# Retention's input projections for all tokens at once by Strassen's scheme, through DRAM

## The chip, the cores and the metric

The kernel runs on one core of a Trainium2 chip. The core's engines work in parallel, each through its own queue in order: PE (TensorE, matmuls), DVE (VectorE), ACT (ScalarE), POOL (GpSimd) and SP (SyncE, which here issues the DMAs). The metric is the device time of one execution in microseconds; less is better. The median of three runs stands for the kernel before: 2782.24 us (2781.03 to 2786.2).

## The reference

A trunk of two layers over 1024 tokens of width 1024, in float32. Layer 0 mixes tokens by sparse attention, layer 1 by retention; behind each stands a gated feed-forward network with a convolution over three tokens. The change is in layer 1's mixer:

```python
proj = h @ w_in                       # h = rms_norm(x), 1024 x 1024; w_in 1024 x 6144
q = rotary(proj[..., :dq].reshape(bsz, seq, B_HEADS, B_DK))          # 4 heads of 256
k = rotary(proj[..., dq:2 * dq]...) * (B_DK ** -0.5)
v = proj[..., 2 * dq:2 * dq + dv].reshape(bsz, seq, B_HEADS, B_DV)   # 4 heads of 512
g = proj[..., 2 * dq + dv:]
...                                   # per head: (q k^T, decayed) v, plus q times a state
ret = rms_norm(ret, out_g)
y = ret * silu(g)
return y @ w_out
```

The rotary step turns the two halves of each q and k by the angle of their token: x1 cos - x2 sin and x1 sin + x2 cos.

## The kernel before

Every float32 product is made of three matmuls. Each operand is split into a rounded high part and the rest (hh and hl, whi and wlo): ACT copies, DVE subtracts; the product is high x high, low x high and high x low (mm3, L123 to L125). Layer 0's feed-forward network, and both layers' in part, already multiply by Strassen's scheme with seven block products for eight: the tokens are halved, the width and the weight's columns too. The first two products (first_products) go to DRAM (pd), the other five (second_products' loop, in ffn_first) add them up; prep_b makes the combined weights on DVE, product (L753) issues the matmuls.

Retention works on one half of 512 tokens after the other, and in a half on four heads. For a head, rotary() projects q and k with proj_T and turns them out of PSUM with cs, the table of cosines and sines; tok_proj() projects v and g, tokens on the partitions. In the core of a head, S = q k^T for four blocks of keys is scaled by the decay and split into sTh and sTl; the value products v,sT follow (in the second half also q times the state, sth and stl); ACT squares the result with a sum, and a chain of single columns through DVE and POOL gives the factor that normalises it (L678 to L683). Sixteen transposes (L710) turn it to y, which is split again and multiplied by wb_out into x. The first half leaves the state k^T v in DRAM for the second; for it k is kept in kf and transposed (L691). Weights come by SP into two raw slots (wraw), in the order of a list (plan_weights), two ahead of their use.

What sets the order is a scheduler that places each engine's instructions in a list; on the chip each engine then takes its list in order and waits on semaphores. In the kernel before, the projections of head n+1 stand in PE's list among the core's steps of head n. Between the two halves of retention stands the beginning of layer 1's feed-forward network on the first half (ffn_whole, a generator); the end of the second half hands over to the rest of it.

Of the kernel before, what the change touches and what calls it, by code (L numbers as in the profile page):

```python
# [5 lines left out]
F32 = mybir.dt.float32  # L6
# [45 lines left out]
class Prog:  # L52
# [4 lines left out]
    def plan_weights(self, phases):  # L57
        i = self.ins
        seq = []
        for ph, a in phases:  # L60
# [3 lines left out]
            elif ph == "outproj":  # L64
                seq += [(i["wa_out"][m], 1024, a == 0) for m in range(8)]
            elif ph == "up":
                seq += [(i["wf_up"][0, c], 1024, True) for c in range(*a)]
            elif ph == "ret":
                for n in range(4):
                    if n == 0:  # L70
                        seq += [(i["wb_qk"][n * 4 + c], 1024, False) for c in range(4)]
                        seq += [(i["wb_vg"][n, 0, kk], 1024, False) for kk in range(4)]
                    seq += [(i["wb_vg"][n, 1, kk], 1024, False) for kk in range(4)]
                    if n < 3:
                        seq += [(i["wb_qk"][(n + 1) * 4 + c], 1024, False) for c in range(4)]
                        seq += [(i["wb_vg"][n + 1, 0, kk], 1024, False) for kk in range(4)]
                    seq += [(i["wb_out"][n, mm], 1024, False) for mm in range(4)]
        self.wseq, self.wready, self.wpos = seq, [], 0

# [479 lines left out]
    def rotary(self, hh, hl, oh, ol, keep=None):  # L559
        nc = self.nc  # L560
        p0 = self.proj_T(hh, hl)
        p1 = self.proj_T(hh, hl)
        cos, sin = self.cs[:, 0], self.cs[:, 1]
        for d, (a, b, op) in enumerate(((p0, p1, ALU.subtract), (p1, p0, ALU.add))):
            u, v = keep[:, d] if keep is not None else self.tmp(), self.tmp()
            nc.vector.tensor_tensor(u, a, cos, ALU.mult)
            nc.vector.tensor_tensor(v, b, sin, ALU.mult)
            nc.vector.tensor_tensor(u, u, v, op)
            nc.scalar.activation(oh[:, d], u, AF.Copy)
            nc.vector.tensor_tensor(ol[:, d], u, oh[:, d].bitcast(F32), ALU.subtract)  # L570

    def tok_proj(self, hh, hl):

        ps = [self.bank() for _ in range(4)]
        for kk in range(4):
            wh, wl = self.weight()
            for j in range(4):
                for k2 in range(2):
                    k = kk * 2 + k2
                    w_h, w_l = wh[:, k2 * 512:(k2 + 1) * 512], wl[:, k2 * 512:(k2 + 1) * 512]  # L580
                    a, b = hh[:, k, j * 128:(j + 1) * 128], hl[:, k, j * 128:(j + 1) * 128]
                    self.mm3(ps[j], a, b, w_h, w_l, k == 0, k == 7)
        return ps

    def retention(self, half, x, h=None, then=None, also=lambda n: None):
        nc = self.nc
        hh, hl = h or self.all_chunks(x, C_GMIX + 8)
        kz = self.l1.tile([128, 4, 4], F32, tag="kz", name="kz")
        kn = self.l1.tile([128, 4, 4], F32, tag="kn", name="kn")
        ke = self.l1.tile([128, 4, 4], F32, tag="ke", name="ke")  # L590
        tok = lambda i: self.tok[half][i]

        def scales():

            r2 = self.small(4)
            nc.vector.tensor_tensor(r2, tok(1), tok(1), ALU.mult)
            for dst, c, w in ((kn, K_A, r2), (kz, K_Z, r2), (ke, K_EG, tok(0))):
                nc.vector.tensor_tensor(dst, self.kc(c, 16).rearrange("p (n j) -> p n j", j=4),
# [730 lines left out]
```

## Time and profile before

| | |
|---|---|
| median of three runs | 2782.24 us |
| profiled execution, its own time | 2783.58 us |
| its span, first to last instruction | 2781.7 us |
| mean granted TensorE clock | 0.976 |
| PE / DVE / ACT busy | 2655.4 / 1866.9 / 1096.2 us |
| DMA, mean over the span | 118 GB/s |

The span lies 1.9 us inside the profiled execution's time. Busy shares are means over stages of different kinds, so the stages are read one by one, by windows. Matmuls overlap: one of 512 columns lasts 0.39 us in the trace while the next starts earlier, so PE's pace is read from a stretch of them. "Idle before" counts the time an engine waited ahead of a group of instructions, and names what ended the wait.

### The profile page before, as it was taken

The page shows a single profiled execution, that of the slowest core. Times are in us where ns is not written, and L with a number is a line of the kernel's source. Part 1 is how long each engine was busy: PE and PEld are TensorE (multiplying, and loading weights), DVE is VectorE, ACT ScalarE, POOL GpSimd, SP SyncE. Part 2 cuts the span into 40 slices and gives each one's busy share as a digit, 9 for nine tenths or more (in the row PEclk, how much of TensorE's full clock was granted, in tenths as well). Part 3 has the DMA queues.
Part 4 walks back from the last instruction along what each step waited for, and adds up shares of the span by engine and source line. Part 5 has one row for each costly group of instructions (what it writes and reads, how often), then busy time and mean ns, then how long its engine had stood idle before and what let it go on. Part 6 is the DMA issues. An engine that isn't in the chain of part 4 may idle for free.

```text
span 2781.7 us, 31410 instructions
## 1 busy us (share of the span) xinstructions
PE 2655.4 (95%) x11888; PEld 2174.3 (78%) x11888; DVE 1866.9 (67%) x2828; ACT 1096.2 (39%) x1552; POOL 265.2 (10%) x193
## 2 busy tenths in 40 slices
PE   8977789998999999999999999999998999999999
PEld 6755567887788877888888888888886888888887
DVE  6889999765988878744544445445447977777632
ACT  6545424663433333323333343323334554454210
POOL 2543234321000000000000000000000000000000
PEclk9988789999999999999999999999999999999999
DMA  5221035204465575422222223223222433337712
GB/s 196 76 73 53 2 98 182 99 20 138 160 212 189 193 261 176 150 63 90 84 84 87 88 83 122 76 84 98 77 76 84 144 107 108 119 106 286 234 59 87
DMA packets 110343, 328.34 MB, mean 118 GB/s; under 512 B 12400, under 2 KB 13808, under 8 KB 110192
## 3 DMA queue, kind: packets, MB, share of 16 engines
q1 hardware_dynamic: 110192, 326.34, 35.6%
q8 instruction: 93, 1.52, 0.2%
q14 instruction: 58, 0.48, 0.1%
HBM read 250.27 MB, written 72.35 MB: 116 GB/s over the span
## 4 chain that ended last, share of the span: by engine, by line
PE 77%; DVE 15%; DMA 4%; issue 2%; ACT 2%; POOL 0%; SPq 0%; DVEq 0%; ACTq 0%; POOLq 0%
PE bank L753 25%; PE bank L123 17%; PE bank L125 17%; PE bank L124 17%; DVE junk L406 5%; DMA gin<-ud 2%; DVE tkb L416 1%; PE bank L534 1%; DVE sc L385 1%; DVE tkt L417 1%; DMA wraw<-in_wf_up 1%; DVE T L731 1%; DVE wlo L731 1%; DVE xo L764 0%; DVE lg L490 0%
## 5 line engine op out<-in xcount | busy, mean ns | idle before, releaser
L87 ACT ACTIVATE whi<-wraw 128x1024 fp32r<-128x1024 f32 (+1 forms) x194 | 205.3, 1058 | 507.7 <-PE bank L124 262.2
L753 PE MATMUL bank<-T,whi 128*128 128x512 f32 x1072 | 337.5, 396 | 21.6 <-ACT T L730 15.0
L753 PE MATMUL bank<-B,whi 128*128 128x512 f32 x1056 | 328.1, 393 | 11.1 <-ACT B L730 4.1
L89 DVE TENSOR_TENSOR wlo<-wraw,whi 128x1024 fp32r<-128x1024 f32 (+1 forms) x151 | 185.8, 1231 | 214.1 <-ACT whi L87 209.0
L124 PE MATMUL bank<-g,whi 128*128 128x512 f32 x704 | 274.1, 390 | 0.0
L123 PE MATMUL bank<-g,whi 128*128 128x512 f32 x704 | 266.5, 392 | 7.5 <-ACT g L730 5.6
L125 PE MATMUL bank<-g,wlo 128*128 128x512 f32 x704 | 272.5, 390 | 0.5 <-DVE wlo L731 0.5
L753 PEld LDWEIGHTS bank<-T,whi 128*128 128x128 f32 x1072 | 203.8, 190 | 71.0 <-ACT T L730 17.1
L730 ACT ACTIVATE whi<-wraw 128x1024 fp32r<-128x1024 f32 (+2 forms) x153 | 145.1, 949 | 267.0 <-PE bank L124 133.1
L753 PEld LDWEIGHTS bank<-B,whi 128*128 128x128 f32 x1056 | 199.9, 190 | 54.8 <-ACT B L730 4.4
L731 DVE TENSOR_TENSOR wlo<-wraw,whi 128x1024 fp32r<-128x1024 f32 (+2 forms) x153 | 165.7, 1083 | 76.5 <-ACT whi L730 76.3
L753 PE MATMUL bank<-T,wlo 128*128 128x512 f32 x536 | 210.3, 394 | 0.0
L753 PE MATMUL bank<-B,wlo 128*128 128x512 f32 x528 | 205.2, 392 | 0.0
L124 PE MATMUL bank<-wlo,hh 128*128 128x512 f32 x512 | 199.3, 389 | 0.0
L125 PE MATMUL bank<-whi,hl 128*128 128x512 f32 x512 | 199.3, 389 | 0.0
L123 PE MATMUL bank<-whi,hh 128*128 128x512 f32 x512 | 198.7, 390 | 0.0
L123 PE MATMUL bank<-hh,whi 128*128 128x512 f32 (+2 forms) x480 | 188.7, 393 | 10.3 <-ACT hh L134 8.3
L124 PE MATMUL bank<-hl,whi 128*128 128x512 f32 (+2 forms) x480 | 186.5, 389 | 0.1
L125 PE MATMUL bank<-hh,wlo 128*128 128x512 f32 (+2 forms) x480 | 186.4, 389 | 0.0
L406 DVE TENSOR_SCALAR_CACHE_REDUCE junk<-sc,tkt 128x640 f16<-128x640 f32 (+1 forms) x192 | 181.3, 944 | 4.4
L764 DVE TENSOR_TENSOR xo<-xo,bank 128x512 f32<-128x512 f32 x128 | 86.7, 685 | 126.8 <-PE bank L125 126.8
L123 PEld LDWEIGHTS bank<-g,whi 128*128 128x128 f32 x704 | 132.2, 188 | 37.6 <-ACT g L730 7.8
(244 smaller groups left out, 5305.6 us busy)
## 6 DMA issues: line engine op xcount, KB each, us to landing
wraw<-in_wf_up SPq DMA_DIRECT2D x113, 512.0 KB, 3.6
ud<-cu SPq DMA_DIRECT2D x88, 512.0 KB, 2.7
gin<-ud SPq DMA_DIRECT2D x88, 512.0 KB, 4.5
wraw<-in_wb_vg SPq DMA_DIRECT2D x64, 512.0 KB, 3.5
wraw<-in_wf_dn SPq DMA_DIRECT2D x48, 384.0 KB, 3.6
wraw<-in_wb_qk SPq DMA_DIRECT2D x32, 512.0 KB, 3.6
wraw<-in_wb_out SPq DMA_DIRECT2D x32, 512.0 KB, 3.5
wraw<-in_wa_in SPq DMA_DIRECT2D x26, 512.0 KB, 4.0
```

Of the source, the lines that this page charges most:

```text
L87: nc.scalar.activation(hi[:, :n], raw[:, :n], AF.Copy)
L89: eng.tensor_tensor(lo[:, :n], raw[:, :n], hi[:, :n].bitcast(F32), ALU.subtract)
L123: mm(ps, ah, bh, start=first, stop=False)
L124: mm(ps, ah, bl, start=False, stop=False)
L125: mm(ps, al, bh, start=False, stop=last)
L385: nc.vector.scalar_tensor_tensor(sc[:, o:o + n], rl[:, :n], w, sc[:, o:o + n], op0=ALU.mult, op1=ALU.add)
L406: V.tensor_scalar(junk[:, :Ls[b]], scs[b], of(b), None, op0=op, op1=ALU.add, accum_out=cnt[:, b:b + 1])
L416: V.tensor_scalar(bit, cnt, TOPK - 0.5, float(1 << k), op0=ALU.is_lt, op1=ALU.mult)
L730: return (self.nc.scalar.activation(hi, raw, AF.Copy), self.nc.vector.tensor_tensor(lo, raw, hi.bitcast(F32), ALU.subtract))
L731: self.nc.vector.tensor_tensor(lo, raw, hi.bitcast(F32), ALU.subtract))
L753: self.nc.tensor.matmul(ps, u, v, start=first and k + i == 0, stop=k == 3 and i == 2, skip_group_check=not (first and last))
L764: self.nc.vector.tensor_tensor(o, a, b, op)
```

## The change

A new function, ret_inputs, computes q, k, v and g for all 1024 tokens between layer 0's feed-forward network and the core. The columns of q, k and g are 16 pairs of 128 and go through first_products and second_products, which is now a function of its own; the values keep the tokens on the partitions, so val_product multiplies with the tokens as the stationary operand, in two pairs of heads (vp). Results stand in DRAM: q, k in gd[0], silu(g) in gd[1], v in vd, products that wait in rp and vp, x in xr. The tokens' norm is now applied to x before the projections. The matmuls of the projections go from 2304 to 2016.

In the core, a head's q, k and v come by DMA into the two raw slots, in turn with the weights; DVE turns q and k out of the raw tile and writes part of it in place, and splits them. The gate is loaded into sg; the normalised result goes to rt by ACT and is multiplied by the gate after the transposes (L806). cs, kh, kl, qh and the others of the pool l1 lie where T1, T2, T4, B22 and T3, the token operands of the scheme, lay before. In layer 0's down projection the last group of weights is run for the first token half and then, loaded again, for the second.

```diff
@@ -66,16 +66,17 @@ plan_weights
             elif ph == "ret":
-                for n in range(4):
...
+                seq += [(self.ret_src(c)[0], 1024, False) for c in range(16)]
+                seq += [(i["wb_vg"][n, 0, kk], 1024, False) for n in (0, 2) for kk in range(4)]
+            elif ph == "retout":
+                seq += [(i["wb_out"][n, mm], 1024, False) for n in range(4) for mm in range(4)]
@@ -556,87 +557,181 @@
-    def rotary(self, hh, hl, oh, ol, keep=None):
+    def ret_inputs(self, x, tt, s3, B):
...
+        for _ in self.first_products(range(16), B, self.rp):
+            next(rest, None)
...
+        for vp in range(2):
+            a = [self.bank() for _ in range(4)]
+            for half in range(2):
+                for q in range(2):
+                    hi, lo = self.weight()
+                    self.val_product(a, hi, lo, B[half], q, half == 0, half == 1)
+                for j in range(4):
+                    t = self.tmp()
+                    nc.scalar.activation(t, a[j], AF.Copy)
+                    nc.sync.dma_start(self.vp[vp][j] if half == 0 else self.vd[2 * vp][0][j], t)
+
+        def done(c, cc):
+            n, j = c // 4, c % 4
+            for i in range(2):
+                if j % 2:
+                    nc.scalar.activation(cc[i], cc[i], AF.Silu)
+                nc.sync.dma_start(self.gd[j % 2][n * 4 + j // 2 * 2 + i], cc[i])
...
+        self.second_products(16, self.ret_src, ops, nxt, s3, self.rp, done)
+
+        for vp in range(2):
+            vs = [self.hp.tile([128, 2, 2048], F32, tag="h", name="va") for _ in range(2)]
...
+            pq = self.xp.tile([128, 8, 512], F32, tag="x", name="vpq")
+            uq = self.xp.tile([128, 8, 512], F32, tag="x", name="vuq")
...
+            def s1(q):
+                add(sl(s3t, q), sl(a11, q), sl(a21, q), ALU.subtract)
+                add(sl(a21, q), sl(a21, q), sl(a22, q))
...
+            s3t = uq[:, 4:].rearrange("p k t -> p (k t)")
...
+            run(d, s1, T1, True, False, lambda j, ps: add(pq[:, 4 + j], ps, pq[:, j]))
+            a = [self.bank() for _ in range(4)]
+            run(a, s2, T2, True, False, lambda j, ps: add(uq[:, j], ps, pq[:, j]))
+            run(d, s4, B22, False, True, give(2 * vp, 1, uq))
+            run(a, lambda q: sl(s3t, q), T3, False, False, give(2 * vp + 1, 1, pq[:, 4:]))
+            run(a, lambda q: sl(a22, q), T4, False, True, give(2 * vp + 1, 0, pq))
...
+    def val_product(self, ps, hi, lo, t, q, first, last):
+        for j in range(4):
+            for k2 in range(2):
+                k = 2 * q + k2
+                w = [v[:, k2 * 512:(k2 + 1) * 512] for v in (hi, lo)]
+                b = [t[:, i, k, j * 128:(j + 1) * 128] for i in range(2)]
+                for i, (u, v) in enumerate(((b[0], w[0]), (b[0], w[1]), (b[1], w[0]))):
+                    self.nc.tensor.matmul(ps[j], u, v, start=first and k + i == 0, stop=k == 3 and i == 2,
+                                          skip_group_check=True)
+
+    def retention(self, half, x, then=None, also=lambda n: None):
...
+        def raw_pair(srcs):
+            raw = self.wp.tile([128, 1024], F32, tag="raw", bufs=2, name="wraw")
+            for t, src in zip(two(raw), srcs):
+                nc.sync.dma_start(t, src)
+            return raw
+
+        def rotary(j, n, oh, ol, keep):
+            add = self.add
+            a, b = two(raw_pair([self.gd[0][n * 4 + j * 2 + d][:, t0:t1] for d in range(2)]))
+            u, v = keep[:, 0] if keep is not None else self.tmp(), self.tmp()
+            add(u, a, cs[:, 0], ALU.mult)
+            add(v, b, cs[:, 1], ALU.mult)
+            add(u, u, v, ALU.subtract)
+            self.split(oh[:, 0], ol[:, 0], u)
+            add(b, b, cs[:, 0], ALU.mult)
+            add(a, a, cs[:, 1], ALU.mult)
+            w = keep[:, 1] if keep is not None else b
+            add(w, b, a)
+            self.split(oh[:, 1], ol[:, 1], w)
...
+            for j in (0, 2):
+                raw = raw_pair([self.vd[n][half][j + i] for i in range(2)])
+                self.split(self.two(v, 0, j), self.two(v, 1, j), raw)
...
-            for j, ps in enumerate(self.tok_proj(hh, hl)):
-                nc.scalar.activation(sg[:, j], ps, AF.Silu, scale=tok(1)[:, j:j + 1])
+            for c in range(4):
+                nc.sync.dma_start(sg[:, c], self.gd[1][n * 4 + c][:, t0:t1])
...
-                nc.vector.scalar_tensor_tensor(sg[:, j], ps, f, sg[:, j], op0=ALU.mult, op1=ALU.mult)
+                nc.scalar.activation(rt[:, j], ps, AF.Copy, scale=f)
@@ -995,13 +1114,16 @@ down
+        if l == 0:
+            todo[-8:] = [(g0, n, m, (h,)) for h in range(2) for g0, n, m, _ in todo[-8:]]
@@ -1204,37 +1348,32 @@ run
             with tt as tt, s3 as s3:
-                x, h = self.ffn_first(x, tt, s3)
+                x, B = self.ffn_first(x, tt, s3)
+                self.ret_inputs(x, tt, s3, B)
...
+                x = [self.xp.tile([128, 8, 512], F32, tag="x", name="x") for _ in range(2)]
+                for h in range(2):
+                    for m in range(8):
+                        nc.sync.dma_start(x[h][:, m], self.xr[h][m])
+                self.retention(0, x[0])
                 last = self.ffn_whole(1, x)
-                self.retention(1, x[1], None, last)
+                self.retention(1, x[1], last, lambda n: self.mean_square(0) if n == 0 else None)
```

Three places in the lists of instructions, row by row. The first is DVE's list where the first half of retention starts. Before, the projections of head 0's k and v (kf out of a bank, L132 v) are turned and split in between the splits of further weights:

```order
L568 TENSOR_TENSOR kf<-kf,t_9916 128x512
L89 TENSOR_TENSOR wlo<-wraw,whi 128x1024
L568 TENSOR_TENSOR kf<-kf,t_9922 128x512
L570 TENSOR_TENSOR kl_9852<-kf,kh_9851 128x512 x2
L89 TENSOR_TENSOR wlo<-wraw,whi 128x1024 x3
L132 TENSOR_TENSOR v<-bank,v 128x512 x4
L641 SCALAR_TENSOR_TENSOR t_10070<-bank,kn,kon 128x128
```

Now there are two stretches. At the end of the columns the results are added into cu, and then value pair 0 begins with vuq (vuq<-va is s3t, wlo<-va the first combined weight):

```order
L860 TENSOR_TENSOR cu<-bank,t_12362 128x512
L860 TENSOR_TENSOR cu<-bank,t_12346 128x512
L860 TENSOR_TENSOR vuq<-va 128x1024 x2
L860 TENSOR_TENSOR va<-va 128x1024 x3
L827 TENSOR_TENSOR wlo<-va,whi 128x1024
L860 TENSOR_TENSOR va<-va 128x1024
L827 TENSOR_TENSOR wlo<-va,whi 128x1024
L860 TENSOR_TENSOR va<-va 128x1024
L827 TENSOR_TENSOR wlo<-va,whi 128x1024
```

and behind the last results of value pair 1 (vpq) head 0's k and q are turned, out of wraw:

```order
L860 TENSOR_TENSOR t_13143<-bank,vpq 128x512
L860 TENSOR_TENSOR t_13146<-bank,vpq 128x512
L860 TENSOR_TENSOR kf<-wraw,cs 128x512
L860 TENSOR_TENSOR t_13183<-wraw,cs 128x512
L860 TENSOR_TENSOR t_13199<-wraw,cs 128x512
L860 TENSOR_TENSOR t_13200<-wraw,cs 128x512
L860 TENSOR_TENSOR wraw<-wraw,cs 128x512
L860 TENSOR_TENSOR kf<-kf,t_13183 128x512
L860 TENSOR_TENSOR wraw<-wraw,cs 128x512 x2
L860 TENSOR_TENSOR t_13199<-t_13199,t_13200 128x512
L860 TENSOR_TENSOR wraw<-wraw,cs 128x512
L860 TENSOR_TENSOR kf<-wraw 128x512
```

The splits of weights that stood among the turns are gone from there, and the turns stand behind the last value results.

The second place is PE's list in the second half, at the end of head 0's value products. Before, the projections of g and the next head's v (hh,whi) and, behind the transposes, its q (whi,hh) stand there:

```order
L123 MATMUL bank<-hh,whi 128x512
L124 MATMUL bank<-hl,whi 128x512
L125 MATMUL bank<-hh,wlo 128x512
L710 MATMUL bank<-kon,sg 128x128 x16
L123 MATMUL bank<-whi,hh 128x512
L124 MATMUL bank<-wlo,hh 128x512
L125 MATMUL bank<-whi,hl 128x512
L123 MATMUL bank<-whi,hh 128x512
```

Now the value products, the transposes and the output products follow each other:

```order
L124 MATMUL bank<-v,sTh_14899 128x512
L125 MATMUL bank<-v,sTh_14899 128x512
L126 MATMUL bank<-v,sTl_14900 128x512
L804 MATMUL bank<-kon,rt 128x128 x16
L124 MATMUL bank<-y,whi 128x512
L125 MATMUL bank<-y,whi 128x512
L124 MATMUL bank<-y,whi 128x512
L125 MATMUL bank<-y,whi 128x512
L126 MATMUL bank<-y,wlo 128x512
```

Nothing stands between the square of the result and its transposes on PE now, nor between those and y's products.

The third place is DVE's list in the second half's head 0. Before, the state's split (stl) is followed by splits of weights and the normalising chain (s, sg):

```order
L135 SCALAR_TENSOR_TENSOR sTl_13240<-bank,kn,sTh_13239 128x128
L644 TENSOR_TENSOR sTl_13255<-t_13256,sTh_13254 128x128
L656 TENSOR_TENSOR stl<-t_13262,sth 128x512
L656 TENSOR_TENSOR stl<-t_13266,sth 128x512
L89 TENSOR_TENSOR wlo<-wraw,whi 128x1024 x4
L680 SCALAR_TENSOR_TENSOR s_13412<-s_13410,ke 128x1
L683 SCALAR_TENSOR_TENSOR sg<-bank,s_13414,sg 128x512
L680 SCALAR_TENSOR_TENSOR s_13433<-s_13431,ke 128x1
```

Now v's last split and the next head's turns (out of wraw) stand around the state's split:

```order
L827 TENSOR_TENSOR v<-wraw,v 128x1024
L860 TENSOR_TENSOR t_15021<-wraw,cs 128x512
L827 TENSOR_TENSOR stl<-t_14907,sth 128x512
L827 TENSOR_TENSOR stl<-t_14911,sth 128x512
L860 TENSOR_TENSOR t_15022<-wraw,cs 128x512
L860 TENSOR_TENSOR wraw<-wraw,cs 128x512
L860 TENSOR_TENSOR t_15038<-wraw,cs 128x512
L860 TENSOR_TENSOR t_15021<-t_15021,t_15022 128x512
L860 TENSOR_TENSOR wraw<-wraw,cs 128x512
```

The turns, which stood in a stretch of their own behind the chain, come ahead of it.

## Rows read from the trace of the kernel before

**Rows 1.** Page: busy time of each engine, and the chain by engine.

```profile
PE 2655.4 (95%) x11888; PEld 2174.3 (78%) x11888; DVE 1866.9 (67%) x2828; ACT 1096.2 (39%) x1552; POOL 265.2 (10%) x193
...
PE 77%; DVE 15%; DMA 4%; issue 2%; ACT 2%; POOL 0%; SPq 0%; DVEq 0%; ACTq 0%; POOLq 0%
```

**Rows 2.** Windows: stretch, length, busy us (instructions) of engines, clock, DMA share, GB/s.

```profile
705.00:990.00 285.00, 285.00 (x1251) 235.75 (x1251) 241.22 (x303) 110.65 (x112) 0.00 (x0) 0.99 0.59 192
990.00:1020.00 30.00, 24.91 (x101) 19.50 (x100) 18.38 (x20) 8.88 (x9) 0.00 (x0) 0.94 0.98 353
1245.00:2092.00 847.00, 844.68 (x3866) 702.74 (x3865) 405.82 (x599) 284.44 (x437) 22.17 (x35) 1.00 0.27 87
2130.00:2160.00 30.00, 24.24 (x90) 17.40 (x91) 28.02 (x34) 17.30 (x22) 0.00 (x0) 0.85 0.11 36
```

**Rows 3.** Groups by line, DVE, 705 to 990: count, busy us, mean ns, idle.

```profile
L859 DVE SCALAR_TENSOR_TENSOR cu<-cu,cols 128x1022 f32<-128x1022 f32 x25 | 32.0, 1280 | 0.0
```

**Rows 4.** Groups by line, PE in 1245 to 2092.

```profile
L123 PE MATMUL bank<-whi,hh 128*128 128x512 f32 x512 | 198.7, 390 | 0.0
L123 PE MATMUL bank<-hh,whi 128*128 128x512 f32 x256 | 99.8, 390 | 0.0
```

**Rows 5.** Timeline at the end of a head's value products: start, length, engine, operation.

```profile
1865.28 0.40 PE L125 MATMUL bank<-v,sTl 128*128 128x512 f32 x1
1865.52 0.39 PE L123 MATMUL bank<-hh,whi 128*128 128x512 f32 x1
...
1865.78 0.60 ACT L678 ACTIVATE t<-bank 128x512 f32<-128x512 f32 x1 [3.46 <-PE bank L125]
...
1866.27 0.19 ACT L678 ACTIVATION_READ_ACCUMULATOR t<-bank 128x1 f32 x1
...
1866.50 0.16 DVE L680 SCALAR_TENSOR_TENSOR s<-s,ke 128x1 f32<-128x1 f32 x1 [1.34 <-ACT t L678]
...
1866.80 0.54 POOL L139 TENSOR_TENSOR s<-s,nh 128x1 f32<-128x1 f32 x1 [2.44 <-DVE s L680]
...
1867.38 0.75 DVE L683 SCALAR_TENSOR_TENSOR sg<-bank,s,sg 128x512 f32<-128x512 f32 x1 [0.72 <-POOL s L139]
```

**Rows 6.** Timeline of DVE on a rotary.

```profile
1887.49 0.69 DVE L567 TENSOR_TENSOR t<-bank,cs 128x512 f32<-128x512 f32 x1 [3.30 <-PE bank L125]
1888.10 0.68 DVE L566 TENSOR_TENSOR t<-bank,cs 128x512 f32<-128x512 f32 x1
```

**Rows 7.** Groups by line and shape in 1245 to 2092: the split of a weight.

```profile
L89 DVE TENSOR_TENSOR wlo<-wraw,whi 128x1024 fp32r<-128x1024 f32 x126 | 154.3, 1225 | 194.2 <-ACT whi L87 192.9
L87 ACT ACTIVATE whi<-wraw 128x1024 fp32r<-128x1024 f32 x125 | 132.9, 1063 | 376.9 <-PE bank L124 203.0 <-PE bank L125 167.5 <-issue 4.5
```

**Rows 8.** DMA issues by kind: count, KB each, median us to landing.

```profile
ud<-cu SPq DMA_DIRECT2D x88, 512.0 KB, 2.7
...
wraw<-in_wb_out SPq DMA_DIRECT2D x32, 512.0 KB, 3.5
...
cs<-in_cossin SPq DMA_DIRECT2D x2, 512.0 KB, 4.1
```

**Rows 9.** DMA issues of the stretch 2510 to 2570.

```profile
gin<-ud SPq DMA_DIRECT2D x18, 512.0 KB, 6.4
...
ud<-cu SPq DMA_DIRECT2D x4, 512.0 KB, 8.0
```

**Rows 10.** Timeline of PE: a head's transposes.

```profile
1887.29 1.91 PE L710 MATMUL bank<-kon,sg 128*128 128x128 f32 x16
```

**Rows 11.** Timeline of PE after a wait.

```profile
1015.68 2.44 PE L123 MATMUL bank<-g,whi 128*128 128x512 f32 x6 [1.92 <-ACT g L730]
1017.92 0.63 PE L124 MATMUL bank<-g,whi 128*128 128x512 f32 x1
1018.35 0.63 PE L125 MATMUL bank<-g,wlo 128*128 128x512 f32 x1
...
1019.89 0.39 PE L125 MATMUL bank<-g,wlo 128*128 128x512 f32 x1
```

More of the change, by code (lines that the diff above doesn't have):

```diff
@@ L572, in tok_proj @@
[L572 to L583, printed above, removed]
@@ new lines, in val_weight @@
+    def val_weight(self, raw):
+        hi = self.wp.tile([128, 1024], F32R, tag="whi", bufs=3, name="whi")
+        lo = self.wp.tile([128, 1024], F32R, tag="wlo", bufs=3, name="wlo")
+        self.split(hi, lo, raw)
+        return hi, lo
+    def val_product(self, ps, hi, lo, t, q, first, last):
+        for j in range(4):
+            for k2 in range(2):
[5 more added lines that the diff above has]
+                                          skip_group_check=True)
@@ new lines, in retention, with qk, values @@
+    def retention(self, half, x, then=None, also=lambda n: None):
+        nc = self.nc
+        self.plan_weights([("retout", 0)])
+        cs = self.l1.tile([128, 2, 512], F32, tag="cs", name="cs")
+        nc.sync.dma_start(cs, self.ins["cossin"][half])
+        t0, t1 = half * H, half * H + H
+        two = lambda t: [t[:, i * 512:(i + 1) * 512] for i in range(2)]
+        def raw_pair(srcs):
[16 more added lines that the diff above has]
+            self.split(oh[:, 1], ol[:, 1], w)
+        def qk(n):
+            kf = self.hp.tile([128, 2, 512], F32, tag="h", name="kf") if half == 0 else None
+            r = []
+            for j in (1, 0):
+                oh = self.l1.tile([128, 2, 512], F32R, tag=("qh", "kh")[j], name=("qh1", "kh1")[j])
+                ol = self.l1.tile([128, 2, 512], F32R, tag=("ql", "kl")[j], name=("ql1", "kl1")[j])
+                rotary(j, n, oh, ol, (None, kf)[j])
+                r = [oh, ol] + r
+            return r + [kf]
+        def values(n):
@@ L886, in finish, with second_products @@
                 nc.sync.dma_start(self.ud[0][1][c], ub)
-        for c in range(NFF):
+        self.second_products(NFF, src, ops[0], nxt[0], s3, self.pd, done)
+        return self.down(0, tt, late)
+    def second_products(self, n, src, ops, nxt, s3, pd, done):
+        nc, add = self.nc, self.add
+        T1, T2, T4, B22, T3 = ops
+        cu = [self.xp.tile([128, 4, 1024], F32, tag="x", name="cu") for _ in range(2)]
+        held = None
+        def finish(p):
+            c, a, a22, p1, cc = p
+            self.product(a, a22, T4, False, True)
+            add(cc[1][:, :512], a, p1)
+            done(c, cc)
+        for c in range(n):
             s1, s2, s3_, s4, a22 = nxt
@@ L1051, in down, with inputs @@
                 nc.sync.dma_start(y[h][:, m], self.xd[l][h][m])
-        hs = None
+        B, more = None, iter(())
         ahead = []
-        for i, (g0, n, m) in enumerate(todo):
+        def inputs():
+            nonlocal B
+            self.mean_square(0)
+            yield
+            chunk = self.normaliser(y[0], C_GMIX + 8, 0)
+            for k in range(4):
+                chunk(k)
+            yield
+            B, ch = self.first_inputs(y[0])
+            next(ch)
+            yield
+            for k in range(4, 8):
+                chunk(k)
+            yield
+            yield from ch
+        for i, (g0, n, m, hs) in enumerate(todo):
             final = g0 + n == NFF
-            lag = l == 0 and final and m > 0
-            if i + 2 < len(todo) and not lag:
+            if i + 2 < len(todo):
                 dn(i + 2)
@@ L1206, in run @@
                     pass
-                for _ in self.first_products(range(NFF - PRE[0]), B):
+                for _ in self.first_products(range(NFF - PRE[0]), B, self.pd):
                     steps(3)
```

250 lines of the change are left out of this document (127 added, 123 removed).

## The prediction

> **What bounds the kernel now.** I read the page's busy shares and chain first [rows 1]: TensorE (PE) is busy for 2655.4 of 2781.7 us and carries 77% of the chain that ended last. The windows say whether that holds in the stages that the change touches [rows 2]. In 705 to 990 us, the old Strassen stage (layer 0's second products), PE is busy for all 285.00 us with 1251 matmuls: 285.00/1251 = 0.228 us from one 512-column matmul to the next. In 1245 to 2092, inside retention, it is busy for 844.68 of 847.00, so 2.3 us are idle, while VectorE (DVE) needs 405.82 and DMA 27%. The groups of that window [rows 4] hold 512 matmuls of the form whi,hh and 256 of hh,whi; each stands there on three lines, 768 x 3 = 2304: all the projections of q, k, v and g. So PE is the bound, the projections cost what their count costs, and they have a second office. The timeline at the end of a head's value products [rows 5] shows it: after the last v,sTl at 1865.28 the chain ACT square, ACT accumulator, DVE, POOL, DVE runs on until 1868.13, and PE spends that time on hh,whi, projection matmuls that need nothing of it.
>
> **What is removed.** 2304 matmuls become 384 + 192 (first products) and 960 + 480 (second products), 2016; 288 fewer x 0.228 = **65.7 us**. New first and second products have the shape of the stage at 705 to 990, where the same additions, splits and stores left PE no idle time, so I cost that arithmetic at nothing; the cover is PE's 60 matmuls (13.7 us) a column, and by DVE's 241.22 busy of 285 there is 15% left. Layer 0's conv, in which a line like that of [rows 3] stands for 32.0 us of that DVE time, is not in the new columns. If the cover fails, a column costs what DVE exceeds 13.7 us. The 2.3 us idle in the window go as well: **68.0 us** in all.
>
> **What is added: waits on PE.** Prices: 512-wide DVE operations in a row start 0.60 us apart (1887.49, 1888.10; the first lasts 0.69) [rows 6]; a 1024-wide one lasts 1.22, and in a row I take 1.14 (0.08 less, as at 512; an estimate); an ACT copy of 1024 lasts 1.06 [rows 7]. A store of 512 KB lands after 2.7 us, a 512 KB weight after 3.5, cs after 4.1 [rows 8]; in the burst of 2510 to 2570 loads of 512 KB take 6.4 and stores 8.0 [rows 9].
>
> (1) Columns to value pair 0. The last column's accumulation ends at E. The first DVE operation of the pair writes vuq, which has the slot of cu; it waits until the last gate's store has left it. Add (0.95 with its lag), two SiLUs of 1024 (2.1, by ACT's copy), then the store, with 2 MB of va loads ahead of it in SP's queue: 3.0 + 8.0 = E+11 by the burst, E+5.7 by the quiet row; I take E+8.5, between them, since half of those loads are released a column earlier. Then five adds before the first wlo, which is what the second matmul of each pair reads: 5 x 1.14 + 1.22 = 6.9, so E+15.4; matmuls that read only whi cover 1.8. **13** (10 to 16).
>
> (2) Pair 0 to pair 1: vuq again, now behind the last add: 0.95 + 6.9 - 1.8 = **6** (5 to 8).
>
> (3) Pair 1 to the core. cs takes the place of T4, which the last value product reads, so its load starts at E2 and lands at E2+4. Sixteen DVE operations of 0.60 follow for head 0's k and q (9.6), with two ACT copies between them: S's products, 3.8 us of PE work, end at E2+16, 12 lost. v's splits hold the value products 2 more. The weights of wb_out come last of all: two raw slots, in order, so they queue behind head 1's k, q and v. From the last ksl split on, DVE needs 7.5 us to free k's slot, 12.1 to q's last split, 13.3 to v's first; the load then freed lands 3.5 later and is split 1.06 later, at 18. PE has 2 us left there (8 matmuls): 16 lost. 12 + 2 + 16 = **30** (26 to 36). No row of before shows a core head without projections, so this is built, not seen.
>
> (4) Heads 1 to 3 of the first half: the state products stand beside the y chain; PE has 150 matmuls of 512 columns (30 value, 24 state, 96 output: 34.2), S 3.8 and 24 transposes at 0.12 (2.9) [rows 10], 40.9 us a head; DVE's operations of a head come to about 34 (rotary 9.6, sT 4.4, v and wlo 6 x 1.2, x 8 x 0.60, y with the gate 8 x 0.65, ksl 2). 2 each, **6** (0 to 12).
>
> (5) Second half, head 0: DVE's rotary stands behind the last x addition, and stl behind the rotary: q,k ends 12.5 after the last matmul and sth's products 21; less what PE does meanwhile, 16.5. The first wb_out weight again comes after v, 10.5 more. **27** (16 to 30).
>
> (6) Second half, heads 1 to 3. The y chain is uncovered: [rows 5] give 0.60 + 0.19 + 0.16 + 0.54 with gaps, 1.6 from the square's start at 1865.78 to the last step's at 1867.38, 0.3 ahead of it, and ACT's copy 0.6 behind it: 2.5; then the sixteen transposes, 1.91 [rows 10], are PE's own work; then DVE's gain, ACT's copy and DVE's rest of y, 1.7 to the first y matmul: 4.2 idle a head. stl now stands behind the rotary, 5.5 a head, in one head also behind eight normaliser operations. 3 x 4.2 + 5.5 + 10.5 = **29** (14 to 38).
>
> (7) Clock. Behind an idle 1.92 us matmuls of 0.63 stood 0.43 apart, and only 4 us later, from 1019.89, did they take 0.39 again [rows 11]; the granted clock of the stretch 990 to 1020 is 0.94, and of 2130 to 2160 0.85 [rows 2], between the levels 1.2 and 2.4 GHz as a mean. I add 1.5 for each of (1), (3) and (5), and 0.5 for the rest: **8** (2 to 14).
>
> Waits: 13 + 6 + 30 + 6 + 27 + 29 + 8 = **119 us** (73 to 154 if all ends come together).
>
> The Trainium skill, "TensorE: Matmul & The Clock Gate", section "HAM oscillation — how this bites in real kernels", says that a kernel whose matmul groups alternate with waits can start every group cold, paying the half clock again each time. The slow matmuls behind the 1.92 us of idle time agree. Without the rule term (7) would be some 3, the three long waits at 1 us each, and the time 2828; with it paid at every wait inside a head, the contention rival below.
>
> Other moves: the last group of layer 0's down projection runs all units of the first token half, then those of the second, with eight more weight loads (as those of 3.5 in [rows 8]) and x0's normalisation beside it. DVE has about 29 us of work there (8 units of 0.9 + 0.6 + 0.6, 8 gains of 0.6, 4 splits and 2 early weights of 1.2) for 33 of PE (144 matmuls): 0, at most 3. The new loads and stores of rp and gd run beside the columns, as pd and ud did at 705 to 990, with DMA at 59% and 192 GB/s there against 353 at 990 to 1020 [rows 2]: 0.
>
> Net: 119 - 68 = +51. Against the profiled execution's own 2783.58: 2834.6; the median of the runs, 2782.24, lies 1.3 under it, so **2833**.
>
> **Rivals.**
> - *Handovers only* (faster). DVE and ACT run ahead inside the core, as the scheduler's order lets them, so (4), (6) and the weights of (3) and (5) cost nothing: 13 + 6 + 14 + 16.5 + 4 = 54 against 68: -14, 2768. For it: DVE is busy for less than half of the retention window [rows 2]. Against it: the y chain is a chain of latencies, whoever has time. It decides if y's weights are split before the transposes end.
> - *All hidden* (faster): 2783.6 - 68 = 2715 or so, if PE finds other work at each place. After the change the order puts the products of the value step, the transposes and the y products next to each other, with nothing between: 1 in 30.
> - *Even*: waits of 63 to 74 us, within 0.2% (5.6 us, what a measurement of this kernel can tell from no change).
> - *Contention and clock* (worse): the 2 MB of x loads, vd, gd and weights at the handovers land at 8 us as in [rows 9], and the core's matmuls run at a mean clock of 0.85 as in 2130 to 2160: 323 x 0.15/0.85 = 57, less the 8 already in: 2833 + 49 = 2882. For it: clock follows waits in [rows 2]. Against: gaps of 2 to 5 us between groups of 20 us.
>
> **How the numbers follow.** Slower as worked out 0.72 (2800 to 2865 alone); contention 0.08; even 0.05; handovers only 0.12; all hidden 0.03. Faster 0.15, same 0.05, slower 0.80. The range takes in the ends of the seven terms and the handover rival: 2766 to 2870.
>
> **What would show it.** In the profile after: a PE busy time lower by 60 to 66 us; PE idle gaps of 10 us or more at three places (before the first value product, before the first S product of each half), each ended by DVE; cs landing after the last value product; PE's L804 waiting for ACT in heads 1 to 3 of the second half; PEclk under 0.9 in slices of the core. Wrong would be: the core's 323 us of matmuls (4 x 40.9 and 4 x 39.9) in less than 345 (then handovers only), or idle gaps within the columns (DVE's cover gone, slower than I say).

## The result, and the profile after

The change makes the kernel slower: median 2872.82 us (2868.34 to 2873.74, 4 runs) against 2783.44, a ratio of 1.0318 (95%: 1.03 to 1.0335). The forecast was 2833 with a range of 2766 to 2870: right in sign, 40 us short, and 2.8 us outside the range. The profiled execution takes 2871.95 us, its span is 2870.2.

The page after, in its busy shares and its granted clock, stands against [rows 1]:

```profile
PE 2631.9 (92%) x11616; PEld 2144.4 (75%) x11616; DVE 2011.2 (70%) x3036; ACT 1134.0 (40%) x1606; POOL 265.0 (9%) x193
...
PEclk9987889999999999999999897998899999999999
```

PE runs 272 matmuls fewer and yet is busy only 23.5 us less, and four slices of the clock row behind the middle stand at 7 or 8. Both runs agree within 0.5 us up to 1076 us and behind the end of retention. The windows of that stage answer to [rows 2] (columns as there), first of the kernel before:

```profile
1076.00:2123.90 1047.90, 1045.04 (x4755) 868.27 (x4753) 540.42 (x757) 350.27 (x514) 23.18 (x36) 1.00 0.30 94
```

Then of the kernel after, the whole stage and its parts (columns by Strassen's scheme; value pairs; first half's core; second half's core):

```profile
1076.00:2212.90 1136.90, 1020.10 (x4482) 836.24 (x4480) 683.24 (x963) 389.77 (x568) 22.86 (x36) 0.94 0.45 149
1240.00:1590.00 350.00, 350.00 (x1553) 289.74 (x1551) 199.38 (x255) 121.76 (x151) 1.01 (x1) 1.00 0.59 194
1590.00:1740.00 150.00, 124.76 (x523) 100.63 (x521) 71.26 (x80) 23.32 (x22) 0.00 (x0) 0.92 0.39 138
1740.00:1965.00 225.00, 179.11 (x792) 146.04 (x792) 136.43 (x236) 89.78 (x164) 9.44 (x16) 0.88 0.39 129
1965.00:2205.00 240.00, 194.86 (x850) 158.24 (x851) 148.85 (x247) 92.50 (x160) 11.41 (x18) 0.90 0.33 107
```

The stage grew by 1136.90 - 1047.90 = 89.0 us, the whole difference. Three sums make it up. **Work**: 1045.04/4755 = 0.2198 us a matmul before, a mean over wide and narrow ones; 4755 - 4482 = 273 fewer give -60.0. **Idle**: 1136.90 - 1020.10 = 116.8 after, 2.9 before: +113.9. **Clock**: 4482 x 0.2198 = 985.0, but PE was busy 1020.10: +35.1, which agrees with the records of the granted clock, half in 14 spells between 1606 and 2125 us that cost 33.6 us of busy time (half of what PE was busy in them; 1.5 to 3.5 each). The records show no such spell in this stretch of the kernel before. 113.9 + 35.1 - 60.0 = 89.0. In the columns PE has no idle time and the full clock: all the loss lies behind 1590.

PE's waits there (us in all, times, longest):

```profile
PE bank L124 <- ACT whi L88: 36.9, 4, 19.8
PE bank L668 <- ACT whi L826: 21.5, 4, 15.5
PE bank L124 <- ACT qh L826: 18.8, 2, 11.3
PE bank L125 <- DVE stl L827: 11.1, 3, 7.5
PE bank L124 <- ACT sth L826: 8.3, 4, 4.0
PE bank L125 <- DVE y L827: 8.3, 6, 3.3
PE bank L124 <- ACT y L826: 6.4, 6, 1.4
PE bank L804 <- ACT rt L777: 3.2, 5, 1.1
```

The releaser that the profile names is often the last link of a chain. The first long wait, in the timeline of all engines (start, length, engine, operation, in brackets the idle time before it and what ended it):

```profile
1600.83 2.23 SPq L609 DMA_DIRECT2D va<-in_wb_vg  x4
...
1603.18 0.35 SPq L599 DMA_DIRECT2D gd<-cu  x1
...
1611.70 2.36 DVE L860 TENSOR_TENSOR vuq<-va 128x1024 f32<-128x1024 f32 x2 [10.17 <-DMA gd<-cu]
...
1616.34 2.07 PE L668 MATMUL bank<-whi,T 128*128 128x512 f32 x4 [15.54 <-ACT whi L826]
```

The last gate's store stands behind four va loads of 512 KB in SP's queue and only when it has left its slot, 8.5 us after its issue began (1611.70 less 1603.18), may DVE write vuq, which lies there. The longest wait, 19.81 us ahead of head 0's output products, and what follows it:

```profile
1785.78 1.23 DVE L827 TENSOR_TENSOR v<-wraw,v 128x1024 fp32r<-128x1024 f32 x1 [2.81 <-ACT v L826]
1786.34 1.06 ACT L826 ACTIVATE v<-wraw 128x1024 fp32r<-128x1024 f32 x1 [0.59 <-DMA wraw<-vd]
1787.03 8.91 SPq L87 DMA_DIRECT2D wraw<-in_wb_out  x4
1790.64 1.06 ACT L88 ACTIVATE whi<-wraw 128x1024 fp32r<-128x1024 f32 x1 [3.25 <-DMA wraw<-in_wb_out]
1791.75 0.80 PE L124 MATMUL bank<-y,whi 128*128 128x512 f32 x1 [19.81 <-ACT whi L88]
...
1792.77 0.63 PE L124 MATMUL bank<-y,whi 128*128 128x512 f32 x1
...
1797.76 0.39 PE L124 MATMUL bank<-y,whi 128*128 128x512 f32 x1
```

The output weight's load is issued at 1787.03, when the first split of head 1's v (DVE, to 1787.01) gives a raw slot back. Behind the wait a matmul lasts 0.63 us until 1797, then 0.39. The windows on both sides show the two levels, 1.2 and 2.4 GHz:

```profile
1791.70:1797.00 5.30, 5.25 (x12) 4.13 (x13) 2.45 (x2) 1.42 (x2) 0.00 (x0) 0.50 0.47 134
1797.00:1805.00 8.00, 8.00 (x36) 6.59 (x35) 4.42 (x5) 1.75 (x2) 0.00 (x0) 1.00 0.56 186
```

### The profile page after: what moved, and what is told of

Its sections match the earlier page's. It is cut to its first block, busy times and chain, and to the rows that moved or that the text cites. A ratio compares the mean times of both kernels' runs of the same rounds, so it can differ in the third digit from the quotient of the medians.

```text
span 2870.2 us, 31665 instructions
## 1 busy us (share of the span) xinstructions
PE 2631.9 (92%) x11616; PEld 2144.4 (75%) x11616; DVE 2011.2 (70%) x3036; ACT 1134.0 (40%) x1606; POOL 265.0 (9%) x193
## 4 chain that ended last, share of the span: by engine, by line
PE 74%; DVE 17%; DMA 4%; issue 2%; ACT 2%; SPq 0%; POOL 0%; DVEq 0%; ACTq 0%; POOLq 0%
PE bank L849 35%; PE bank L125 11%; PE bank L126 10%; PE bank L124 10%; DVE junk L407 5%; PE bank L668 5%; DMA gin<-ud 1%; DVE tkb L417 1%; DVE t L860 1%; PE bank L535 1%; DVE tkt L418 1%; DMA wraw<-vd 1%; DVE x L835 1%; DVE sc L386 1%; DMA wraw<-in_wf_up 1%
## 5 line engine op out<-in xcount | busy, mean ns | idle before, releaser
L849 PE MATMUL bank<-B,whi 128*128 128x512 f32 x1440 | 445.4, 392 | 11.1 <-ACT B L826 4.1
L849 PE MATMUL bank<-T,whi 128*128 128x512 f32 x1344 | 419.5, 394 | 23.9 <-ACT T L826 16.0
L88 ACT ACTIVATE whi<-wraw 128x1024 fp32r<-128x1024 f32 (+1 forms) x122 | 128.5, 1053 | 260.0 <-PE bank L125 90.4
L849 PE MATMUL bank<-T,wb 128*128 128x512 f32 x864 | 213.9, 391 | 0.8 <-DVE cu L860 0.8
L860 DVE TENSOR_TENSOR cu<-bank,t 128x512 f32<-128x512 f32 x198 | 133.9, 686 | 112.4 <-PE bank L849 107.3
L849 PEld LDWEIGHTS bank<-T,wb 128*128 128x128 f32 x864 | 163.1, 189 | 35.3 <-DVE cu L860 1.2
L90 DVE TENSOR_TENSOR wlo<-wraw,whi 128x1024 fp32r<-128x1024 f32 (+1 forms) x79 | 97.6, 1238 | 115.6 <-ACT whi L88 112.0
L124 PEld LDWEIGHTS bank<-g,whi 128*128 128x128 f32 x704 | 132.1, 188 | 35.6 <-ACT g L826 6.5
L849 PEld LDWEIGHTS bank<-B,wlo 128*128 128x128 f32 x720 | 135.9, 189 | 28.3
L126 PEld LDWEIGHTS bank<-g,wlo 128*128 128x128 f32 x704 | 132.1, 188 | 28.6 <-DVE wlo L827 1.0
L125 PEld LDWEIGHTS bank<-g,whi 128*128 128x128 f32 x704 | 132.1, 188 | 27.5
```

The lines of the kernel that those rows point to most:

```text
L88: nc.scalar.activation(hi[:, :n], raw[:, :n], AF.Copy)
L90: eng.tensor_tensor(lo[:, :n], raw[:, :n], hi[:, :n].bitcast(F32), ALU.subtract)
L124: mm(ps, ah, bh, start=first, stop=False)
L125: mm(ps, ah, bl, start=False, stop=False)
L126: mm(ps, al, bh, start=False, stop=last)
L849: self.nc.tensor.matmul(ps, u, v, start=first and k + i == 0, stop=k == 3 and i == 2, skip_group_check=not (first and last))
```

## The experiments

Two theories stood against each other. *Waits*: each wait has its own cause in the order of a queue or in the reuse of a piece of memory, goes when that is undone, and the half clock is a second price of the same waits. *DVE and ACT as the bound*: behind 1590 DVE and ACT are the limit, and a wait taken away comes back at the next place. Ratios are to the kernel before, with 95% intervals; gains are to the changed kernel's 2872.8.

**One wait at a time.** a_s3late: S3 is made late and in place, so that the first DVE operation of a value pair no longer writes vuq.

```diff
-                add(sl(s3t, q), sl(a11, q), sl(a21, q), ALU.subtract)
...
+            def s3(q):
+                add(sl(a11, q), sl(a22, q), sl(a11, q), ALU.subtract)
+                return sl(a11, q)
```

> Value pairs only: S3 is no longer written first into the slot of cu (vuq) but made later, as a22 - S2 in place; nothing is left out. Theory W (the loss is PE's named waits, each with a spell of half clock behind it): the 15.5 us wait ahead of value pair 0 falls under 4 and its spell (3.2 us of PE time) goes with it, the 5.5 us wait ahead of pair 1 changes by less than 3; 2857 us (2850 to 2862). Rival (the burst of weight loads behind the columns is what is late, whatever DVE writes first): the wait stays at 10 or more, 2866 or above.

2848.36 us (2846.25 to 2850.76), 1.0229 [1.0212, 1.0246]: -24.5, more than expected, since the wait of 5.5 us ahead of pair 1 went too. The waits of L668 (21.5) are gone from the list whole; only 2.9 us came back, in two small waits (for cu and for sTh), and the half clock costs 4.8 us less (28.9). The window of the value pairs, 1590 to 1740, to set beside that of after:

```profile
1590.00:1740.00 150.00, 134.40 (x584) 110.28 (x583) 89.31 (x117) 33.79 (x46) 1.48 (x2) 0.94 0.50 175
```

b_wfirst: two output weights are loaded ahead of the next head's q and k, and v behind the second.

```diff
+            self.prefetch(self.wpos + 2)
             if n < 3:
...
-            if n < 3:
-                nxtv = values(n + 1)
             for mm in range(4):
                 wh, wl = self.weight()
+                if mm == 1 and n < 3:
+                    nxtv = values(n + 1)
```

> Core only: the first two output weights of a head are loaded and split ahead of the next head's k and q, and the next head's v after the second output weight is in use. Theory W: PE's waits for output weights (38.5 us in six) fall under 10, and some 6 us of half clock go: 2838 us (2828 to 2848). Rival D (the core is bound by DVE's and ACT's work, a wait removed comes back at the next one): the waits for q,k and y rise by as much as those for weights fall, 2862 or above.

2848.81 (2847.35 to 2852.08), 1.0232 [1.0217, 1.0247]: -24. Its PE waits:

```profile
PE bank L668 <- ACT whi L827: 21.3, 4, 15.4
PE bank L124 <- ACT qh L827: 18.5, 2, 11.1
PE bank L125 <- DVE stl L828: 10.9, 2, 7.5
PE bank L125 <- DVE y L828: 10.8, 5, 3.7
PE bank L124 <- ACT sth L827: 9.6, 4, 5.3
PE bank L805 <- ACT rt L777: 8.7, 7, 3.0
PE bank L124 <- ACT y L827: 7.8, 8, 1.4
PE bank L124 <- ACT sTh L738: 3.5, 3, 2.2
```

The 36.9 us of L88 are gone, but rt's waits grew by 5.5, y's by 2.5 and 1.4, sth's by 1.3, sTh's from nothing to 3.5: 14.2 came back in these rows, and the half clock costs only 4.3 less. The gain is less than *waits* gave and more than the other theory.

d_state: the state goes into rt's tile as soon as that is free, instead of through two small ones, so that its split can stand ahead of the next head's turns.

```diff
-                    st = self.tmp()
-                    nc.sync.dma_start(st, self.state[n * 2 + d])
-                    self.split(sth[:, d], stl[:, d], st)
+                    nc.sync.dma_start(rt[:, d], self.state[n * 2 + d])
+                    self.split(sth[:, d], stl[:, d], rt[:, d])
```

> Second half only: the state is loaded into the result's tile (rt) as soon as that is free instead of a temporary, so its split can stand ahead of the next head's turns. Theory W: the waits for sth and stl (8.3 + 11.1 us) fall under 6, with some 4 us of half clock: 2855 us (2850 to 2862). Rival D: other waits of those heads take the place, 2867 or above.

2861.92 (2858.61 to 2863.02), 1.0276 [1.026, 1.0291]: -11, at the slow end of what was expected. The 19.4 us of sth and stl went; the waits for rt rose from 3.2 to 15.3. So the waits at a handover went nearly whole in a_s3late, and of those inside a head a part came back (14.2 of 36.9 us, 12.1 of 19.4), at the next link of DVE's and ACT's chain.

**The clock by itself.** Useless matmuls fill the six longest waits: 256 of them (e_junk), 324 (e2_long, with operands that are free at once), 487 with the shorter waits too (e2_all). These are the counts of the edits and of the traces; the expectations of e_junk, e2_all and g_full give 40, 10 and 10 fewer. The useless matmuls write a PSUM bank ahead of the product that uses it.

```diff
+    def junk(self, ps, a, b, n, behind=None):
+        mm = lambda: self.nc.tensor.matmul(ps, a, b, start=True, stop=True)
...
+                    if m == 0:
+                        self.junk(ps, sT[0][0][:, :128], sT[0][0], ((90, 0, 0, 0), (52, 0, 0, 0))[half][n], tr)
```

> 216 matmuls of 512 columns whose results are overwritten are added, 49 us of PE time at full clock, inside the six longest waits (55, 20, 40, 75, 26 and 40 of them, each block shorter than its wait). The result is as before. Theory W with the clock as a term of its own: the waits end when they did, PE stays at 2.4 GHz through them, and the spells behind these six (16 us together) go: 2858 us (2853 to 2863). Rival C (the half clock does not come from the waits but from the narrow products and transposes of the core): 2870 to 2876; if the blocks are late or hold up the loads, above that.

> The useless matmuls again, on operands that nothing waits to overwrite (in e_junk those of the core read v, whose tile the next head's v needs, which held up the weight loads behind it) and as many as fill the six longest waits wholly: 72, 24, 52, 90, 34 and 52, 74 us of PE time. Theory W with the clock as a term of its own: the spells of half clock behind these six (15 us together) go, up to 4 us are lost where a block is longer than its wait: 2861 us (2856 to 2867). Rival C (the half clock does not come from the waits): 2871 to 2880.

> As e2_long, and the shorter waits of the core filled as well (ahead of sth, of y, and of the second output weight: 153 matmuls more, 35 us). Theory W: no wait of more than 2 us is left in the core, the half clock there falls from 33.6 us of lost PE time to under 8, at a cost of up to 8 us where blocks are longer than waits: 2852 us (2845 to 2860). Rival C: 2871 to 2885.

e_junk: 2875.87 (2872.75 to 2877.02), 1.0326 [1.031, 1.0341], a miss. Its junk read v, whose tile the next head's v takes, so it held back loads, and waits of 2 to 7 us were left: its time tells nothing on the clock, though the half clock fell to 23.7. e2_long: 2863.57 (2860.55 to 2865.34), 1.0287 [1.0272, 1.0302], -9; half clock costs 15.1. e2_all: 2849.56 (2847.96 to 2852.58), 1.0239 [1.0224, 1.0254], **-23**. Its window from 1590 to the end of the core, and PE's waits in it:

```profile
1590.00:2181.00 591.00, 575.86 (x2633) 470.81 (x2631) 354.88 (x561) 203.00 (x344) 21.60 (x33) 1.00 0.38 127
```

```profile
PE bank L125 <- DVE y L848: 5.6, 8, 1.3
PE bank L820 <- ACT rt L793: 4.6, 7, 1.5
```

PE does some 107 us of work that nobody needs (487 x 0.22) in place of 101 us of idle time, and the kernel is faster because the half clock costs 1.7 us instead of 33.6. So the clock is a term of its own, of about 30 us, and the waits bring it on.

**All known causes together.** abcdf: a, b and d, with cs in a tile of its own and head 0's rotary in free memory. abcdfh: besides, the second half's first q, k and v are made beside the first half's last output products.

```diff
-        cs = self.l1.tile([128, 2, 512], F32, tag="cs", name="cs")
+        cs = self.hp.tile([128, 2, 512], F32, tag="h", name="cs")
...
+            elif half == 0:
+                cs = turned(1)
+                nxt = qk(0, 1, cs)
```

> a_s3late, b_wfirst and d_state together, cs loaded into a tile of its own ahead of the core, and head 0's turns of the first half with memory that is free before the last value product. Theory W (waits add): -24 -24 -11 as measured alone, and the 11.3 us wait for q,k with its spell of 3.5 falls to 4: -11; 2802 us (2792 to 2815). Rival D (bound by DVE's work, gains shared): 2820 or above.

> As abcdf, and the second half's first q, k and v are loaded, turned and split beside the first half's last output products. Theory W: the 7.5 us wait for q,k of the second half, what is left of the wait for sth, and a spell go: 12 us less than abcdf, 2790 us (2778 to 2804). Rival D: as abcdf within 4 us.

abcdf: 2796.49 (2794.53 to 2799.25), 1.0048 [1.0033, 1.0063], -76. abcdfh: 2791.14 (2787.33 to 2792.77, 7 runs), 1.0025 [1.0013, 1.0036], -82; that is 5 less than abcdf and not 12, since the wait of 7.5 for q,k went, but those for y (11.2 in abcdf) and acc (0.5) grew. Window and waits of abcdfh:

```profile
1590.00:2125.00 535.00, 491.57 (x2188) 402.46 (x2187) 356.26 (x566) 204.34 (x347) 32.88 (x34) 0.94 0.43 142
```

```profile
PE bank L124 <- ACT y L857: 15.1, 8, 4.7
PE bank L832 <- ACT rt L801: 11.4, 10, 4.1
...
PE bank L125 <- DVE y L858: 8.4, 4, 2.7
PE bank L181 <- DVE acc L175: 3.9, 1, 3.9
```

43.4 us are idle (535.00 - 491.57) and 0.9 in the columns, against 2.9 in the kernel before: +41.4. The half clock costs 24.7, and the work is 60.0 less: +6.1, where the two profiled executions differ by 5.6 (2789.18 and 2783.58). The account of after holds with other waits in it.

**What is left inside a head.** g_ms (the mean square one head later), g_full (166 useless matmuls on top), i_late (q and k of the next head turned only behind the split of y), i_junk (74 more), j_mixms (i_late's order in the first half, abcdfh's in the second, mean square and its use one head later), j_junk (53 more). The edits of g_ms, of i_late and of j_mixms:

```diff
-                self.retention(1, x[1], last, lambda n: self.mean_square(0) if n == 0 else None)
+                self.retention(1, x[1], last, lambda n: self.mean_square(0) if n == 1 else None)
```

```diff
             for mm in range(4):
                 wh, wl = self.weight()
+                if mm == 0:
+                    with self.tc.issue_after(ylast.ins):
+                        if n < 3:
+                            nxt = qk(n + 1, half, cs)
```

```diff
+            if half and n < 3:
+                nxt = qk(n + 1, half, cs)
+            elif then and n == 3:
                 next(then)
...
-                if mm == 0:
+                if mm == 0 and half == 0:
```

> As abcdfh, with the mean square of the first half's output taken one head later, so that PE does not wait 3.9 us for its sum (acc). Theory W: that wait and its spell of 1.7 go: 2786 us (2781 to 2790). Rival D: 2789 to 2793.

> As g_ms, with 156 useless matmuls (36 us at full clock) in the waits that are left in the core: ahead of S of the first half, of the transposes of the second, and of y. Theory W with the clock as a term of its own: of the 25 us that half clock still costs in abcdfh's core some 20 go, blocks longer than their waits cost up to 6: 2770 us (2763 to 2778), faster than the kernel before the change (2783.6). Rival (the blocks hold up the transposes by what they save): 2783 to 2790.

> As abcdfh, with the next head's q and k turned behind the split of y instead of ahead of it, beside the output products. Theory W (order, not work, bounds the core): PE's waits for y (15.1 + 8.4 us) fall under 10 and the spells behind them go, no other wait grows by more than 4: 2771 us (2763 to 2780), faster than the kernel before (2783.6). Rival D (DVE's and ACT's work bounds the core, 47 us a head whatever the order): waits for q,k and sT take their place, 2784 or above.

> As i_late, with 74 useless matmuls (17 us at full clock) ahead of S and of y. Theory W with the clock as a term of its own: 2 to 10 us less than i_late, 2765 us (2757 to 2776). Rival (the blocks cost what they save, as in g_full): i_late or up to 6 more.

> The order of i_late in the first half (turns behind the split of y), that of abcdfh in the second (turns ahead of it, so that the fourth output weight does not queue behind k and q), and the mean square of the first half's output with its use one head later each. Theory W (every wait has its own cause in the order): first-half heads of 42 to 44 us as in i_late, second-half heads of 52, 52 and 47 as in abcdfh, no wait for acc of 5.5 us: 2770 us (2763 to 2777). Rival D (DVE's and ACT's work bounds the second half): second-half heads of 54 us or more, 2780 or above.

> As j_mixms, with 53 useless matmuls (12 us at full clock) ahead of S and of y, none longer than the wait it fills. Theory W with the clock as a term of its own: of the spells left (some 15 us in the core) a half goes: 2764 us (2757 to 2772). Rival (no gain where the waits are a few us, as between i_late and i_junk): within 3 us of j_mixms.

g_ms: 2791.44 (2789.52 to 2793.62), 1.003 [1.0019, 1.0042], a miss: acc's 3.9 went, and one wait of 8.6 for rms stands in its place. g_full: 2795.2 (2792.03 to 2798.35), 1.0046 [1.0032, 1.006], a miss: against g_ms the first half became 6.8 us shorter and the second, up to its last output product, 9.7 longer, where 70 useless matmuls kept PE busy 17.6 us longer and took away 7.9 us of idle time. i_late: 2783.57 (2782.08 to 2788.3, 11 runs), 0.9999 [0.9991, 1.0008], level with the kernel before, but not the gain expected. The time is that of the other theory, but not the waits it named (q,k and sT). PE's waits:

```profile
PE bank L124 <- ACT whi L88: 16.3, 4, 5.1
PE bank L124 <- ACT y L859: 7.7, 8, 1.2
...
```

First-half heads take 44.1, 42.2 and 42.3 us from one S to the next, against 47.5 to 56 in abcdfh and 40.9 of work by the prediction's count; in the second half output weights are late by 3.3 to 5.1 a head. Hence the mixture: j_mixms, **2774.64** (2771.59 to 2779.97, 8 runs), 0.9972 [0.9962, 0.9983], 8.6 us faster than the kernel before and 98 faster than the changed one. Its parts behind the columns (value pairs; first and second half's core):

```profile
1590.00:1720.00 130.00, 125.93 (x545) 103.95 (x544) 82.86 (x99) 26.72 (x27) 0.00 (x0) 0.98 0.51 175
1720.00:1910.00 190.00, 180.13 (x853) 148.07 (x852) 144.31 (x258) 95.08 (x179) 8.60 (x16) 0.99 0.51 163
1910.00:2110.00 200.00, 179.10 (x802) 146.33 (x801) 128.39 (x212) 82.75 (x142) 23.03 (x18) 0.92 0.35 111
```

Its waits from 1590 to 2105:

```profile
PE bank L829 <- ACT rt L801: 17.2, 9, 4.1
PE bank L124 <- ACT y L861: 7.4, 8, 1.4
```

The first half's core now runs at a clock of 0.99 and 95% busy; 34.8 us of idle time and 15.5 of half clock are left, most of both in the second half. i_junk: 2785.22, 1.0007 [0.9998, 1.0016], a miss. j_junk: 2772.92 (2770.71 to 2777.32), 0.9965 [0.9953, 0.9978], not to be told from j_mixms, though its half clock costs 10.0 and not 15.5. Once the waits were short, useless matmuls gave nothing measurable.

## Why the prediction was right in direction and wrong in size

**Removed (65.7 + 2.3).** 288 matmuls of 512 columns went as worked out, and at full clock such matmuls start 0.227 us apart (the median) in this stage of both traces, so their price was right. The sums above show 60.0 of work and 2.9 of idle time less: the forecast was 5 us too much. The normaliser got 16 short ones (kon,rms: 32 before, 48 after), some 2 us by [rows 10], which was not counted. And a matmul counts as busy for 0.39 us, though in a row the next one starts after 0.23: each of the 38 waits in the stage (7 before) has 0.16 us of the pause in the busy time, some 5 us in all, an estimate. The cover in the columns held: 350.00 busy of 350.00.

**Idle time (terms 1 to 6: 111 us).** Measured 116.3 from 1590 to 2205 us (615.00 less 498.73 busy). By terms, forecast in brackets: (1) 15.8 (13); (2) 5.7 (6); (3) 31.9 (30), of which 11.3 and 0.8 on q and k, and 19.8 on the output weight; (4) 15.4 (6, upper end 12); (5) 24.0 (27); (6) 22.7 (29); 0.8 more stand at the end of the columns. The parts agree within 3 us for (1) to (3), and with their causes: a_s3late takes (1) and (2) away through vuq alone, b_wfirst the output weight's share of (3) and (5) through the order of the raw slots. In (4) I had counted DVE's work against PE's as totals; the waits for y and for a late output weight in heads 1 and 2, 0.9 to 3.3 each, do not appear in totals. (5) and (6) were set too high: the transposes waited for rt 3.2 us in all, not 2.5 a head. The chain took as long as forecast, but twelve of the sixteen transposes need only the first three parts of the result, and in heads 0, 2 and 3 of the second half PE runs them while the chain of the fourth goes on; here in head 2:

```profile
2116.22 1.48 PE L804 MATMUL bank<-kon,rt 128*128 128x128 f32 x12
...
2118.77 0.66 PE L804 MATMUL bank<-kon,rt 128*128 128x128 f32 x4 [1.07 <-ACT rt L777]
```

**Clock (term 7: 8 us, 2 to 14).** This is the step that failed: it measures 33.6 us by the clock records and 35.1 by the pace, four times the term. I paid 1.5 us at three long waits and 0.5 at the rest. The trace shows 14 spells of half clock at 2.4 on average, and the short waits inside heads bring the same price as the long ones: a later output weight of head 2, 2.89 us late in the timeline of PE, starts its products like the one that was 19.81 late:

```profile
1907.09 0.80 PE L124 MATMUL bank<-y,whi 128*128 128x512 f32 x1 [2.89 <-ACT whi L88]
```

e2_all shows that it comes with the waits and is not a by-product of something else; there, with no wait of more than 1.5 us left, one spell remains. The idle time was 5 us over, the removed work 5 under, the clock 26 over: together 36 of the 37 us by which the profiled execution lies above the 2834.6 forecast for it.

The Trainium skill, "TensorE: Matmul & The Clock Gate", section "HAM oscillation — how this bites in real kernels", says that a kernel of alternating groups and waits can start every group cold. The 14 spells behind waits agree. I had put that rule, paid at every wait inside a head, to the contention rival with 0.08: its clock half took place, with a mean of 0.88 and 0.90 over the core's windows, against its 0.85. Its DMA half did not decide: the last gate's store did take 8.5 us, but held PE up only through the slot that vuq takes, as a_s3late shows, and the output weights were late by their place behind q, k and v, as b_wfirst shows.

**Rivals and signs.** *Handovers only*, *all hidden* and *even* fell with the 116 us of idle time. Of the signs named, these came: cs issued at 1737.16 behind the last value product (SP's timeline), PEclk under 0.9 in the core's slices, no idle time within the columns, L804 waiting for ACT, though only 3.2 us. Two came otherwise: PE's busy time fell by 23.5, not 60 to 66, because half-clock matmuls count as busy; and there were four idle gaps over 10 us, not three (15.5, 11.3, 19.8, 11.3), with ACT's split named as the releaser, DVE or a DMA one link behind it. The second half's first S product waited only 7.5. The wait ahead of head 0's output products, the longest of all, stood in terms (3) and (5) but not in the list of signs.

Left open in part: what holds the second half's heads at 47 to 55 us in j_mixms. rt's waits name ACT behind POOL's step of the y chain. At the longest of them the trace shows DVE ahead of both: its one-column step (L798, 0.15 us) starts 4.6 us behind ACT's sum, in its queue behind the next head's turns and the splits of B (the feed-forward network's operand).

```profile
2007.52 0.19 ACT L796 ACTIVATION_READ_ACCUMULATOR rt<-bank 128x1 f32 x1
...
2008.87 2.35 DVE L862 TENSOR_TENSOR B<-x,B 128x1024 fp32r<-128x1024 f32 x2
...
2012.34 0.15 DVE L798 SCALAR_TENSOR_TENSOR s<-s,kon 128x1 f32<-128x1 f32 x1
...
2013.60 0.90 PE L829 MATMUL bank<-kon,rt 128*128 128x128 f32 x4 [4.13 <-ACT rt L801]
```

No run changed that order alone. How far the cut in arithmetic could be taken with every wait gone was not reached: the work is 60 us less, and the best kernel here keeps 8.6 of it.

## What to carry to other kernels

A stage that saves arithmetic by moving work ahead takes away what another stage filled its waits with: count, for each wait behind it, what PE would still have to do there, link by link in each queue and not by totals. Where PE was never idle before, price every new wait, those of 2 to 3 us too, with its idle time and on top the half clock behind it from a row of the same trace. And of such waits first undo those that come from the order of a queue or from reused memory: here three small edits of that kind, with two more of their sort, gave back 76 of 89 us.

## What was not expected of the hardware

A spell of half clock cost 1.5 to 3.5 us whether the wait ahead of it was 2.89 or 19.81 us, so its price went by the number of the waits more than by their length: 33.6 us of clock on 116 of idle time. And 487 matmuls that nobody needs made the kernel 23 us faster, where waits were long; on kernels whose waits were down to 6 us and less, 53 and 74 of them changed nothing that 5 or 11 runs can tell.
